# Gate and up products of the second token group in seven block products for eight

## The chip, the cores and the metric

One core of a Trainium2 chip runs the whole program in one launch. The metric is the device time of one launch in microseconds (us), lower is better. Each core has TensorE (PE, with its weight loads PEld), VectorE (DVE), ScalarE (ACT), GpSimd (POOL) and SyncE (SP), and 16 DMA engines that the queues of all of them feed. Every engine takes its instructions in order and waits on semaphores.

## What is computed

One layer of a streaming encoder on 1024 prompt tokens and 32 sample tokens (1056 columns of width D = 1024). Cut to what matters here:

```python
mix = concat([mlstm(h), fox_attention(h), gmlp(h)]) @ w_o
x = layer_norm(ALPHA * x + (1 + g1) * mix, ln1_g, ln1_b)
h = x * (1 + sc2) + sh2
y = (silu(h @ w_gate) * (h @ w_up)) @ w_down      # w_gate, w_up: 1024 x 2816; w_down: 2816 x 1024
x = layer_norm(ALPHA * x + (1 + g2) * y, ln2_g, ln2_b)
```

All of it is in 32-bit floats.

## The kernel before

Tokens lie on the free axis, features on the 128 partitions. The tokens form two groups, group 0 of 512 columns (two cuts of 256) and group 1 of 544 (two cuts of 272; its last 32 columns are the sample tokens): `GN`, `MM`, `LN`. A function's argument `c` is the group.

**Products.** Every matrix product is taken in three matmuls (`gemm`, L110 to L116): an operand is split into a rounded part `hi` and a rest `lo`, both of the type fp32r, and hi x hi, hi x lo and lo x hi are summed in PSUM. `weights()` (L91 to L106) loads 128 x 1024 floats into a `raw` buffer (3 of them, `RAW`), ACT casts it to `whi` (L102), DVE subtracts to `wlo` (L103; 3 buffers of each, `WB`). Activations are split likewise: `hh`/`hl` in the tiles `ah` and `al`, one pair for each cut, written by `ln1` (ACT L944, DVE L945).

**The FFN.** `w_gate` and `w_up` are cut into 22 tiles of 128 columns. `up(c, j)` computes tile j: for each cut a gate product into the PSUM pool `pg` (buffers `up_g`) and an up product into `pu` (`up_u`), 8 blocks of 128 rows x 3 matmuls each, so 4 x 24 = 96 matmuls of 272 columns a tile for group 1. Then ACT does Exp, Ln, Exp (silu's sigmoid) and DVE two multiplications (L990, L991), and `acth`/`actl` are split off (ACT L992, DVE L993). Tiles come in `GROUPS` of 3 or 4; after a group's tiles `down(c, g)` multiplies with its part of `w_down` and DVE adds each result to the residual `z` (L923). The first tile of the next group comes ahead of each down pass, to cover its start.

**Order in time** (`run`). Group 0's tiles and down passes are woven into the second half of the mixers (eight attention heads "fox", four "mlstm" heads; some 440 to 960 us of the span), since these leave PE free; POOL does the key sums `fm_qkr` (L365), the residual scaling of group 0's first LayerNorm (L954) and the mlstm heads' `mqb`, `mv`, `mo` there. SP issues all loads and stores in one queue (L85, L88). At some 905 us group 1's output projection and its `ln1` follow, from 1013 group 1's FFN pass: tiles 0 to 3, group 0's last LayerNorm (`ln2`, both cuts after tile 3), the down pass, and so on. The last group runs half by half: up products of cut 0, down of cut 0, `ln2` of cut 0, then the same for cut 1, with the gate and up weights loaded and split again. `last_weights` keeps the last part of `w_down` in the chip for both halves.

A scheduler turns the program's order into an order for each engine: a program text that is written in another order, or has more instructions, moves instructions on all of them. `issue_after` holds an instruction behind another one.

## Time and profile before

| what | value |
| --- | --- |
| runs | 1435.03, 1435.16, 1438.75 us (median 1435.16) |
| profiled execution | 1436.1 us, of it span 1434.3 us |
| mean granted PE clock | 0.986 |
| PE / DVE / ACT / POOL busy | 97% / 67% / 45% / 18% of the span |
| moved by DMA | 207.35 MB, mean 145 GB/s |

The profile's times count from the start of the span; a row names the line of the code, the engine, the operation, what it writes and reads, and how often, with its busy time and the mean of one in ns. PE's matmuls are pipelined: the mean of one overlaps with its neighbours, and the count in a stretch gives the pitch.

### The profile page before, as it was taken

The page shows a single profiled execution, that of the slowest core. Times are in us where ns is not written, and L with a number is a line of the kernel's source. Part 1 is how long each engine was busy: PE and PEld are TensorE (multiplying, and loading weights), DVE is VectorE, ACT ScalarE, POOL GpSimd, SP SyncE. Part 2 cuts the span into 40 slices and gives each one's busy share as a digit, 9 for nine tenths or more (in the row PEclk, how much of TensorE's full clock was granted, in tenths as well). Part 3 has the DMA queues.
Part 4 walks back from the last instruction along what each step waited for, and adds up shares of the span by engine and source line. Part 5 has one row for each costly group of instructions (what it writes and reads, how often), then busy time and mean ns, then how long its engine had stood idle before and what let it go on. Part 6 is the DMA issues. An engine that isn't in the chain of part 4 may idle for free.

```text
span 1434.3 us, 28877 instructions
## 1 busy us (share of the span) xinstructions
PE 1385.6 (97%) x11141; PEld 1336.3 (93%) x11141; DVE 960.7 (67%) x2220; ACT 641.3 (45%) x1405; POOL 254.3 (18%) x295
## 2 busy tenths in 40 slices
PE   7999999999999899999999999999999999999994
PEld 4899988989899889999999998999999999999994
DVE  5558655678688777687767765668857545454676
ACT  3323244434445564546555353436745342424353
POOL 0103100043157300000000002254500000000433
PEclk9999999999999999999999999999999999999997
DMA  9754678565654755443443533522224222222431
GB/s 359 253 210 128 200 206 259 160 197 168 224 176 151 215 161 178 115 145 120 126 139 104 101 104 67 196 89 74 100 73 153 89 89 89 89 89 89 133 104 63
DMA packets 120867, 207.35 MB, mean 145 GB/s; under 512 B 21380, under 2 KB 76300, under 8 KB 120728
## 3 DMA queue, kind: packets, MB, share of 16 engines
q1 hardware_dynamic: 120728, 205.49, 45.9%
q8 instruction: 88, 1.44, 0.4%
q14 instruction: 51, 0.42, 0.1%
HBM read 173.78 MB, written 31.66 MB: 143 GB/s over the span
## 4 chain that ended last, share of the span: by engine, by line
PE 82%; DMA 7%; DVE 6%; ACT 1%; issue 1%; SPq 1%; POOL 1%; DVEq 0%; ACTq 0%; POOLq 0%
PE up_g L115 8%; PE up_g L116 8%; PE up_g L114 8%; PE dn_g L114 4%; PE dn_g L115 4%; PE dn_g L116 4%; PE up_u L116 3%; PE up_u L115 3%; PE up_u L114 3%; PE tm_g L279 2%; PE tm_g L280 2%; PE tm_g L281 2%; PE fox_t L729 2%; PE wo_g L114 2%; PE wo_g L115 2%; PE wo_g L116 2%
## 5 line engine op out<-in xcount | busy, mean ns | idle before, releaser
L114 PE MATMUL up_g<-wo_ah,up_whi 128*128 128x256 f32 (+1 forms) x1008 | 288.8, 287 | 3.4 <-ACT lna_tmp L942 3.3
L115 PE MATMUL up_g<-wo_al,up_whi 128*128 128x256 f32 (+1 forms) x1008 | 290.4, 288 | 0.4 <-DVE wo_al L945 0.4
L116 PE MATMUL up_g<-wo_ah,up_wlo 128*128 128x256 f32 (+1 forms) x1008 | 289.4, 287 | 0.0
L114 PEld LDWEIGHTS up_g<-wo_ah,up_whi 128*128 128x128 f32 x1008 | 191.4, 190 | 4.9 <-ACT wo_ah L944 3.5
L115 PEld LDWEIGHTS up_g<-wo_al,up_whi 128*128 128x128 f32 x1008 | 191.6, 190 | 1.3 <-DVE wo_al L945 0.7
L116 PEld LDWEIGHTS up_g<-wo_ah,up_wlo 128*128 128x128 f32 x1008 | 191.3, 190 | 0.4 <-DVE up_wlo L103 0.2
L102 ACT CAST up_whi<-up_raw 128x1024 fp32r<-128x1024 f32 x94 | 98.5, 1047 | 143.1 <-PE dn_u L115 53.8
L103 DVE TENSOR_TENSOR up_wlo<-up_raw,up_whi 128x1024 fp32r<-128x1024 f32 x94 | 121.1, 1288 | 61.0 <-ACT up_whi L102 60.7
L114 PE MATMUL dn_g<-up_acth,dn_whi 128*128 128x256 f32 (+1 forms) x464 | 133.8, 289 | 2.4 <-DVE mlstm_z L923 2.4
L115 PE MATMUL dn_g<-up_actl,dn_whi 128*128 128x256 f32 (+1 forms) x464 | 132.3, 286 | 0.0
L116 PE MATMUL dn_g<-up_acth,dn_wlo 128*128 128x256 f32 (+1 forms) x464 | 132.1, 285 | 0.0
L116 PE MATMUL up_u<-wo_ah,up_wlo 128*128 128x272 f32 (+1 forms) x400 | 115.4, 289 | 0.0
L114 PE MATMUL up_u<-wo_ah,up_whi 128*128 128x272 f32 (+1 forms) x400 | 114.9, 287 | 0.0
L115 PE MATMUL up_u<-wo_al,up_whi 128*128 128x272 f32 (+1 forms) x400 | 114.5, 286 | 0.0
L280 PE MATMUL tm_g<-tm_wlo,start_h1h 128*128 128x256 f32 (+1 forms) x384 | 111.3, 291 | 0.0
L281 PE MATMUL tm_g<-tm_whi,start_h1l 128*128 128x256 f32 (+1 forms) x384 | 111.0, 290 | 0.0
L279 PE MATMUL tm_g<-tm_whi,start_h1h 128*128 128x256 f32 (+1 forms) x384 | 110.3, 289 | 0.2 <-ACT tm_mixs L630 0.2
L114 PE MATMUL fm_g<-start_h1h,fm_whi 128*128 128x256 f32 (+2 forms) x344 | 102.7, 304 | 5.5 <-ACT fm_whi L102 1.9
L115 PE MATMUL fm_g<-start_h1l,fm_whi 128*128 128x256 f32 (+2 forms) x344 | 102.5, 298 | 0.1
L116 PE MATMUL fm_g<-start_h1h,fm_wlo 128*128 128x256 f32 (+2 forms) x344 | 101.4, 296 | 0.0
L114 PEld LDWEIGHTS dn_g<-up_acth,dn_whi 128*128 128x128 f32 x464 | 87.7, 189 | 3.3 <-DVE mlstm_z L923 3.0
L115 PEld LDWEIGHTS dn_g<-up_actl,dn_whi 128*128 128x128 f32 x464 | 87.8, 189 | 0.4
(447 smaller groups left out, 3806.2 us busy)
## 6 DMA issues: line engine op xcount, KB each, us to landing
up_raw<-w_gu SPq DMA_DIRECT2D x94, 512.0 KB
dn_raw<-w_dn SPq DMA_DIRECT2D x30, 512.0 KB
ada_late<-w_ada SPq DMA_DIRECT2D x24, 512.0 KB
wo_raw<-w_o SPq DMA_DIRECT2D x24, 512.0 KB
ada_araw<-w_ada SPq DMA_DIRECT2D x16, 512.0 KB
fm_raw<-w_in_f SPq DMA_DIRECT2D x16, 512.0 KB
tm_raw<-w_in SPq DMA_DIRECT2D x12, 512.0 KB
dn_raw<-w_dn SPq DMA_DIRECT2D x16, 384.0 KB
```

The costliest lines, as they stand in the source:

```text
L102: nc.scalar.copy(hi[:, :w], raw[:, :w])
L103: (eng or nc.vector).tensor_tensor(lo[:, :w], raw[:, :w], f(hi[:, :w]), ALU.subtract)
L114: nc.tensor.matmul(ps, hi, xh(k), start=start and k == 0, stop=False)
L115: nc.tensor.matmul(ps, hi, xl(k), start=False, stop=False)
L116: nc.tensor.matmul(ps, lo, xh(k), start=False, stop=stop and k == n - 1)
L279: nc.tensor.matmul(ps[:, :ncol], xh, hi, start=k == 0, stop=False)
L280: nc.tensor.matmul(ps[:, :ncol], xh, lo, start=False, stop=False)
L281: nc.tensor.matmul(ps[:, :ncol], xl, hi, start=False, stop=k == 7)
L729: nc.tensor.transpose(ps[:, y * P:(y + 1) * P], probs[y][:, b * P:(b + 1) * P], self.ident)
```

## The change

Each gate and up pair of tile j is a product of a 2 x 2 block matrix of weights (rows 0 to 511 and 512 to 1023; gate columns and up columns) with a 2 x 2 block matrix of activations (the same rows; the two cuts). For group 1 and tiles 4 to 21 the change computes it by a scheme of seven block products (`sup`): 7 x 4 x 3 = 84 matmuls of 272 columns for 96. It needs three sums of weight blocks, and four combinations of the activations.

- The input `w_gu` holds for each tile the four blocks gate rows 0 to 511, gate rows 512 to 1023, up rows 0 to 511, up rows 512 to 1023, 512 columns each, side by side.
- `sums` makes the weight sums in DRAM, in `dp[j]` (128 x 4 x 512 for each tile): two copies from DRAM to DRAM of 512 KB, issued on SP (L92 of the changed code, the `store`), then three accumulating transfers in POOL's queue (L1017: 512, 256 and 256 KB), each of which waits for the one before. With `NS0 = 22` all of them are called in group 0's pass, one call after each tile of group 0, copies one step and additions up to three steps behind.
- `sup_operand` makes the four activation combinations: `ln1` of group 1 also stores its result in DRAM (`dh`, 16 stores on SP); after tile 3, 16 loads of 136 KB bring it back, with 32 DVE and 16 ACT operations; the combinations lie in the tiles `ah`/`al` that group 0 no longer needs.
- A new tile loads and splits 3.5 x 1024 columns of weights (two own blocks whole, one more own block, four blocks of sums) in place of 2 x 1024.
- Exp, Ln and Exp work on 544 columns; so does the tail of `sup` on DVE.
- Group 0's `ln2` cuts come after tiles 1 and 2. In the last group the new tiles 19 to 21 are done whole, then the two halves' down passes and LayerNorms; the weights of all four units of that down pass are loaded ahead of both.

```diff
+FF = 22
+SJ = 4
+NS0 = 22
...
+            if c:
+                self.store(self.dh[:, k, sl], h)
...
+    def sums(self):
+        nc = self.nc
+        i = self.nsum
+        self.nsum += 1
+        add = lambda out, x: nc.gpsimd.dma_start(out, x, accum_op=ALU.add)
+        blocks = lambda j: self.d["w_gu"][j].rearrange("p (b n) -> p b n", b=4)
+        if i < FF:
+            b = blocks(i)
+            with self.tc.issue_after(self.lastload.ins):
+                self.store(self.dp[i][:, 0:2], b[:, 2:3].to_broadcast([P, 2, 512]))
+                self.store(self.dp[i][:, 2:4], b[:, 0:2])
+        j = i - 1
+        if SJ <= j < FF:
+            add(self.dp[j][:, 0:2], blocks(j)[:, 0:4:3])
+        j = i - 2
+        if SJ <= j < FF:
+            add(self.dp[j][:, 2], self.dp[j][:, 1])
+        j = i - 3
+        if SJ <= j < FF:
+            add(self.dp[j][:, 3], self.dp[j][:, 2])
...
+    def sup_operand(self, ks):
...
+        for k in ks:
+            for r in (k, k + 4):
+                for t in (0, 272):
+                    x = self.t(self.p2, [P, 272], F32, "tmp", 4)
+                    self.load(x, self.dh[:, r, t:t + 272])
...
+            nc.vector.tensor_tensor(b22, b22, b12, ALU.subtract)
+            nc.vector.tensor_tensor(b12, b11, b12, ALU.subtract)
+            nc.vector.tensor_tensor(b11, b22, b11, ALU.add)
+            nc.vector.tensor_tensor(b21, b11, b21, ALU.subtract)
+            for i, x in ((1, b11), (0, b12), (2, b22), (3, b21)):
+                nc.scalar.copy(self.T[i][0][:, k], x)
+                nc.vector.tensor_tensor(self.T[i][1][:, k], x, f(self.T[i][0][:, k]), ALU.subtract)
...
+    def sup(self, j, act, pool):
...
+        w1 = self.weights(self.d["w_gu"][j][:, :1024], KT, P)
+        w2 = [self.t(self.px, [P, 512], F32R, x, 1) for x in ("w2h", "w2l")]
...
+        w3, w4 = (self.weights(self.dp[j][:, i:i + 2].rearrange("p b n -> p (b n)"), KT, P) for i in (2, 0))
...
+        nc.scalar.copy(u1, prod(w1[:4], own(0, 0)))
+        tt(x[:, a], prod(w1[4:], own(0, 4)), u1, ALU.add)
+        tt(uv[:, a], u1, prod(w3[:4], com(1)), ALU.subtract)
+        tt(uv[:, b], prod(w4[4:], com(0)), uv[:, a], ALU.add)
+        tt(x[:, b], prod(w3[4:], own(272, 4)), uv[:, b], ALU.add)
+        s = self.t(self.p2, [P, 544], F32, "sil", 2)
+        nc.scalar.activation(s, x, AF.Exp, scale=-1.0)
+        nc.scalar.activation(s, s, AF.Ln, bias=self.one)
+        nc.scalar.activation(s, s, AF.Exp, scale=-1.0)
+        tt(s, x, s, ALU.mult)
+        tt(two(c), prod(w4[:4], com(2)).unsqueeze(1).to_broadcast([P, 2, 272]), two(uv), ALU.add)
+        tt(c[:, a], prod(blocks(w2, 0), com(3)), c[:, a], ALU.add)
+        nc.vector.scalar_tensor_tensor(c, c, -1.0, s, ALU.mult, ALU.mult)
+        nc.scalar.copy(ah, c)
+        tt(al, c, f(ah), ALU.subtract)
...
+                if j >= SJ:
+                    self.sup(j, act, pa)
+                    continue
                 weave(self.up(1, j, act, pa, MM[1]))
+                if 0 < j < 3:
+                    self.ln2(0, self.st0, *LN[0][j - 1], "vpvvpvvp", "aaaaaaaa")
+                if j == 3:
+                    weave(self.sup_operand(range(4)))
...
         for half, (a, b) in enumerate(LN[1]):
-            for j in range(j0 + 1 + (half and UPF), j0 + nj):
-                weave(self.up(1, j, (act, act2)[half], pa, ((a, b),)))
...
+            self.down(1, last, act, ((a, b),), st, w)
             self.ln2(1, st, a, b, TADD[half], TAFF[half])
```

What this does to the engines' orders, at three places. POOL, in the start of the mixers' second half (the residual scaling of group 0's LayerNorm, L954, in the changed code L962, and the key sums, L365, now L371), before:

```order
114 L954 TENSOR_SCALAR mlstm_z_837_4328<-mlstm_z_837_4328,start_colp_88 128x256 [waits Activation_49] x4
115 L365 TENSOR_TENSOR fm_qkr_6143<-fm_qkh_6141,fm_qkl_6142 128x272 [waits DMAHW2_49,DVE_49]
116 L370 COPY start_qks_137<-fm_qkr_6143 128x32 [waits Pool_49]
117 L365 TENSOR_TENSOR fm_qkr_6184<-fm_qkh_6182,fm_qkl_6183 128x272 [waits DMAHW2_49,DVE_49]
118 L954 TENSOR_SCALAR mlstm_z_837_4328<-mlstm_z_837_4328,start_colp_88 128x256 [waits Activation_49] x2
```

The same place after (`start_dp_13` is `dp[4]`, the sums of the first new tile; DMASW is the semaphore of a transfer in POOL's queue, DMAHW of one of SP's):

```order
112 L371 TENSOR_TENSOR fm_qkr_6128<-fm_qkh_6126,fm_qkl_6127 128x272 [waits DMAHW7_49,DVE_49]
113 L1017 DMA start_dp_13_69<-w_gu 128x2x512 [waits DMAHW3_49]
114 L945 TENSOR_TENSOR mlstm_z_856_4347<-mlstm_z_856_4347,wo_qs_5375 128x256 [waits DVE_49] x2
115 L962 TENSOR_SCALAR mlstm_z_856_4347<-mlstm_z_856_4347,start_colp_107 128x256 [waits Activation_49]
116 L1017 DMA start_dp_13_69<-start_dp_13_69 128x512 [waits DMAHW4_49,DMASW0_49]
117 L962 TENSOR_SCALAR mlstm_z_856_4347<-mlstm_z_856_4347,start_colp_107 128x256 [waits Activation_49] x3
118 L371 TENSOR_TENSOR fm_qkr_6162<-fm_qkh_6160,fm_qkl_6161 128x272 [waits DMAHW2_49,DVE_49]
119 L371 TENSOR_TENSOR fm_qkr_6203<-fm_qkh_6201,fm_qkl_6202 128x272 [waits DMAHW2_49,DVE_49]
120 L376 COPY start_qks_156<-fm_qkr_6162 128x32 [waits Pool_49]
121 L962 TENSOR_SCALAR mlstm_z_856_4347<-mlstm_z_856_4347,start_colp_107 128x256 [waits Activation_49]
122 L1017 DMA start_dp_13_69<-start_dp_13_69 128x512 [waits DMASW1_49]
```

Three additions with waits of their own stand between instructions that followed each other directly.

SP, the loads around group 1's first down pass and the tiles after it, before:

```order
700 L85 DMA dn_raw_14516<-w_dn 128x768 [waits DMAHW0_49,DVE_49]
701 L85 DMA dn_raw_14568<-w_dn 128x768 [waits DMAHW1_49,DVE_49]
702 L85 DMA dn_raw_14620<-w_dn 128x768 [waits DMAHW2_49,DVE_49]
703 L85 DMA dn_raw_14672<-w_dn 128x768 [waits DMAHW3_49,DVE_49]
704 L85 DMA up_raw_14726<-w_gu 128x1024 [waits DMAHW4_49,DVE_49]
705 L85 DMA up_raw_14732<-w_gu 128x1024 [waits DMAHW5_49,DVE_49]
```

After (`sup_tmp` are the loads for the combinations; `sup_raw` of numbers 15048 to 15066 are the weights of tile 5, the second new one):

```order
777 L88 DMA sup_tmp_14662<-start_dh_68 128x272 [waits DMAHW1_49,DVE_49,Activation_49]
778 L88 DMA sup_raw_15060<-start_dp_14_70 128x1024 [waits DMAHW2_49,DMASW5_49,DMAHW5_49,DMASW4_49,DVE_49]
779 L88 DMA sup_tmp_14664<-start_dh_68 128x272 [waits DVE_49]
780 L88 DMA sup_tmp_14666<-start_dh_68 128x272 [waits DMAHW4_49,DVE_49]
781 L88 DMA sup_raw_15066<-start_dp_14_70 128x1024 [waits DMAHW7_49,DMASW3_49,DVE_49]
782 L88 DMA sup_tmp_14668<-start_dh_68 128x272 [waits DMAHW6_49,DVE_49]
783 L88 DMA sup_tmp_14682<-start_dh_68 128x272 [waits DVE_49,Activation_49]
784 L88 DMA sup_tmp_14684<-start_dh_68 128x272 [waits DMAHW0_49,DVE_49]
785 L88 DMA sup_tmp_14686<-start_dh_68 128x272 [waits DMAHW1_49,DVE_49]
786 L88 DMA sup_tmp_14688<-start_dh_68 128x272 [waits DMAHW2_49,DVE_49]
```

The loads of the last combinations stand behind weight loads of a later tile, in a queue that held weights alone.

DVE, one tile in the middle of group 1's pass, before:

```order
1773 L990 TENSOR_TENSOR up_sil_15516<-up_g_15466,up_sil_15516 128x272
1774 L991 TENSOR_TENSOR up_sil_15516<-up_u_15491,up_sil_15516 128x272
1775 L993 TENSOR_TENSOR up_actl_15453<-up_sil_15516,up_acth_15452 128x272
1776 L103 TENSOR_TENSOR up_wlo_15593<-up_raw_15590,up_whi_15592 128x1024
1777 L990 TENSOR_TENSOR up_sil_15574<-up_g_15524,up_sil_15574 128x272
1778 L991 TENSOR_TENSOR up_sil_15574<-up_u_15549,up_sil_15574 128x272
1779 L103 TENSOR_TENSOR up_wlo_15717<-up_raw_15714,up_whi_15716 128x1024
1780 L993 TENSOR_TENSOR up_actl_15453<-up_sil_15574,up_acth_15452 128x272
```

After, one new tile (its last operation, on 544 columns, comes behind the next tile's first ones, as row 1826 does here):

```order
1824 L107 TENSOR_TENSOR sup_wlo_15803<-sup_raw_15800,sup_whi_15802 128x1024
1825 L1094 TENSOR_TENSOR sup_uv_15690<-sup_tmp_15688,sup_u_15720 128x272
1826 L1107 TENSOR_TENSOR sup_actl_15527<-sup_c_15555,sup_acth_15526 128x544
1827 L1095 TENSOR_TENSOR sup_uv_15690<-sup_g_15734,sup_uv_15690 128x272
1828 L1096 TENSOR_TENSOR sup_sil_15689<-sup_u_15748,sup_uv_15690 128x272
1829 L107 TENSOR_TENSOR sup_wlo_15815<-sup_raw_15812,sup_whi_15814 128x1024
1830 L1103 TENSOR_TENSOR sup_c_15691<-sup_g_15767,sup_uv_15690 128x544
1831 L107 TENSOR_TENSOR sup_wlo_15821<-sup_raw_15818,sup_whi_15820 128x1024
1832 L1104 TENSOR_TENSOR sup_c_15691<-sup_u_15781,sup_c_15691 128x272
1833 L1074 TENSOR_TENSOR sup_w2l_15807<-sup_raw_15808,sup_w2h_15806 128x512
1834 L1101 TENSOR_TENSOR sup_sil_15762<-sup_sil_15689,sup_sil_15762 128x544
1835 L1105 SCALAR_TENSOR_TENSOR sup_c_15691<-sup_c_15691,sup_sil_15762 128x544
```

Eight operations become thirteen, with three and a half weight splits among them in place of two.

More of the change, by code (lines that the diff above doesn't have):

```diff
@@ L84, in load, with weights @@
     def load(self, out, in_):
-        return self.nc.sync.dma_start(out, in_)
+        self.lastload = self.nc.sync.dma_start(out, in_)
+        return self.lastload
     def store(self, out, in_):
         self.nc.sync.dma_start(out, in_)
-    def weights(self, src, nk, ncol, eng=None):
+    def weights(self, src, nk, ncol, eng=None, keep=None):
         nc = self.nc
@@ L975, in up @@
         ah, al = act[j] = [self.t(pool, [P, GN[c]], F32R, x, 5) for x in ("acth", "actl")]
-        w = [self.weights(self.d["w_gu"][2 * j + i], KT, P) for i in range(2)]
+        w = [self.weights(self.d["w_gu"][j][:, i * 1024:(i + 1) * 1024], KT, P) for i in range(2)]
         for a, b in cuts:
@@ L1067, in run @@
         self.dd0 = t([4, 9], "dd0")
+        self.dh = t([P, KT, GN[1]], "dh")
+        self.dp = {j: t([P, 4, 512], f"dp{j}") for j in range(SJ, FF)}
+        self.T = []
+        self.nsum = SJ
         self.dmix = [t([P, KT, GN[c]], f"dmix{c}") for c in range(2)]
@@ L1233, in run @@
         act = {}
-        for g, (j0, nj) in enumerate(GROUPS[:-1]):
-            for j in range(j0 + (g > 0), j0 + nj + 1):
-                weave(self.up(1, j, act, pa, MM[1]))
-            if g == 0:
-                for a, b in LN[0]:
-                    self.ln2(0, st, a, b, "vpvvpvvp", "aaaaaaaa")
-            st = self.ln_begin(nc.gpsimd, sum=False) if g == last - 1 else None
-            self.down(1, g, act, MM[1], st)
+        self.px = self.pool("px")
+        for g, (j0, nj) in enumerate(GROUPS):
+            for j in range(j0 + (g > 0), j0 + nj + (g < last)):
+                if self.nsum < FF + 3:
+                    self.sums()
+                if j >= SJ:
+                    self.sup(j, act, pa)
+                    continue
+                weave(self.up(1, j, act, pa, MM[1]))
+                if 0 < j < 3:
+                    self.ln2(0, self.st0, *LN[0][j - 1], "vpvvpvvp", "aaaaaaaa")
+                if j == 3:
+                    weave(self.sup_operand(range(4)))
+            if g < last:
+                st = self.ln_begin(nc.gpsimd, sum=False) if g == last - 1 else None
+                self.down(1, g, act, MM[1], st)
         st.update(pivot=False, sum=True, order=(4, 5, 6, 7, 0, 1, 2, 3))
-        j0, nj = GROUPS[-1]
         n = nj * 256
```

63 lines of the change are left out of this document (51 added, 12 removed).

## Prediction

> **What bounds the kernel now.** First the head of the page: the busy shares, the slices and the DMA kinds.
>
> ```profile
> PE 1385.6 (97%) x11141; PEld 1336.3 (93%) x11141; DVE 960.7 (67%) x2220; ACT 641.3 (45%) x1405; POOL 254.3 (18%) x295
> DVE  5558655678688777687767765668857545454676
> POOL 0103100043157300000000002254500000000433
> PEclk9999999999999999999999999999999999999997
> DMA  9754678565654755443443533522224222222431
> q1 hardware_dynamic: 120728, 205.49, 45.9%
> PE 82%; DMA 7%; DVE 6%; ACT 1%; issue 1%; SPq 1%; POOL 1%; DVEq 0%; ACTq 0%; POOLq 0%
> ```
>
> TensorE is busy for 97% of the span and carries 82% of the chain that ended last, at full clock. So matmuls taken out are worth their time, if nothing else then ends last. From slice 28 on (group 1's FFN pass) DVE stands at 4 to 5 tenths and the DMA engines at 2: room for the added work, on average. All data moves through one kind of queue, which the hardware issues; there is no row for a DMA from POOL's queue, for one from DRAM to DRAM, or for one that accumulates.
>
> Second the stretches of the span (us, busy and count of PE, PE's loads, DVE, ACT, POOL; clock, DMA share, GB/s): six of group 1's FFN pass, then the stages from which POOL and SP get new work, then the end.
>
> ```profile
> 1013.00:1062.00 49.00, 49.00 (x393) 48.95 (x392) 30.08 (x53) 28.67 (x62) 11.54 (x11) 1.00 0.25 80
> 1062.00:1080.00 18.00, 18.00 (x141) 17.84 (x140) 17.31 (x42) 10.18 (x19) 2.44 (x3) 1.00 0.45 144
> 1080.00:1092.00 12.00, 12.00 (x98) 12.00 (x98) 11.97 (x28) 5.20 (x10) 2.44 (x3) 1.00 0.35 124
> 1150.00:1175.00 25.00, 25.00 (x202) 25.00 (x201) 10.32 (x17) 11.10 (x21) 0.00 (x0) 1.00 0.28 86
> 1200.00:1225.00 25.00, 25.00 (x202) 25.00 (x201) 11.19 (x20) 8.89 (x15) 0.00 (x0) 1.00 0.28 96
> 1300.00:1325.00 25.00, 25.00 (x202) 25.00 (x202) 10.03 (x16) 10.88 (x20) 0.00 (x0) 1.00 0.28 85
> 440.00:465.00 25.00, 24.96 (x193) 24.42 (x192) 20.43 (x40) 15.01 (x32) 17.29 (x18) 1.00 0.43 140
> 465.00:480.00 15.00, 11.25 (x81) 10.56 (x80) 14.79 (x30) 7.95 (x19) 9.12 (x11) 0.89 0.61 190
> 480.00:500.00 20.00, 20.00 (x158) 19.05 (x158) 10.91 (x31) 10.80 (x27) 5.24 (x10) 0.91 0.92 246
> 520.00:860.00 340.00, 339.52 (x2800) 334.60 (x2793) 255.40 (x646) 179.26 (x438) 5.71 (x13) 1.00 0.44 127
> 1392.00:1415.00 23.00, 22.64 (x181) 22.42 (x180) 18.17 (x43) 11.45 (x24) 8.34 (x9) 1.00 0.15 50
> 1415.00:1434.00 19.00, 1.19 (x4) 0.68 (x4) 11.06 (x24) 5.25 (x10) 4.58 (x6) 0.60 0.17 60
> ```
>
> In group 1's pass PE never stops and does 202 matmuls of 272 columns in 25 us: 123.8 ns each. (A group's mean of 288 ns overlaps its neighbours; the pitch is the price.) In 465 to 480 PE stands still for a quarter of the time and in 480 to 500 the DMA engines are at 0.92: that is where new transfers have no room.
>
> **The saving.** Each of the 18 tiles does 84 matmuls for 96: 216 x 0.1238 = 26.7 us less PE time. A tile takes 84 x 0.1238 = 10.40 us in place of 11.88.
>
> **DVE inside a new tile.** Durations from group 1's stretch, 960 to 1434:
>
> ```profile
> L103 DVE TENSOR_TENSOR up_wlo<-up_raw,up_whi 128x1024 fp32r<-128x1024 f32 x53 | 69.8, 1316 | 46.6 <-ACT up_whi L102 46.6
> L102 ACT CAST up_whi<-up_raw 128x1024 fp32r<-128x1024 f32 x53 | 55.5, 1046 | 99.6 <-PE dn_u L115 53.8 <-PE up_g L115 30.8 <-PE up_u L115 5.1
> L990 DVE TENSOR_TENSOR up_sil<-up_g,up_sil 128x272 f32<-128x272 f32 (+1 forms) x48 | 21.0, 438 | 35.3 <-ACT up_sil L989 33.6
> L993 DVE TENSOR_TENSOR up_actl<-up_sil,up_acth 128x272 fp32r<-128x272 f32 (+1 forms) x48 | 22.2, 462 | 11.6 <-ACT up_acth L992 11.5
> L988 ACT ACTIVATE up_sil<-up_sil,start_ones 128x272 f32<-128x272 f32 (+1 forms) x48 | 25.1, 522 | 1.4
> L923 DVE SCALAR_TENSOR_TENSOR wo_z<-dn_u,start_mod,wo_z 128x240 f32<-128x240 f32 (+2 forms) x72 | 26.6, 399 | 21.8 <-PE dn_u L116 20.3 <-POOL wo_z L920 1.3
> L938 DVE TENSOR_TENSOR wo_z<-wo_z,wo_pv 128x272 f32<-128x272 f32 x16 | 8.2, 574 | 0.0
> L945 DVE TENSOR_TENSOR wo_al<-lna_tmp,wo_ah 128x272 fp32r<-128x272 f32 x16 | 7.6, 500 | 0.2 <-ACT wo_ah L944 0.2
> ```
>
> Between 272 columns (438 ns) and 1024 (1316 ns) lies 1.17 ns a column, so 544 columns come to about 755 ns and 512 to 718: estimates from these two rows. Before, a tile has 2 splits of 1316 and 6 operations of about 450 ns: 5.3 us. After, 3 splits of 1024 (3.95), one of 512 (0.72), five operations of 272 (2.2) and four of 544 (3.0) make 9.9 us, 95% of PE's 10.40. ACT has 3 x 1046, 0.6, 0.4 for the copy of the first product, three passes and a cast of 544 (2.5 to 3): under 7 us, hidden. The loads grow from 1 MB to 1.75 MB a tile; 86 GB/s went with a share of 0.28, so 1.75 MiB (1.83 MB) in 10.4 us, 176 GB/s, is a share near 0.57: hidden.
> With DVE at 95% PE waits only where order and buffers let it; three raw and three split buffers and three or more PSUM tiles a pool give DVE a few microseconds of lag. I take 0.2 us a tile, 4 us in all; from 0 to 14 (0.8 us a tile, if the added SBUF-to-SBUF operations cost what L938's 574 ns costs against 438, and each end of a tile is waited for).
>
> **The combinations of the activations.** Sixteen loads, 32 DVE operations (16 as L938 and 16 as L945: 9.2 + 8.0 = 17.2 us) and 16 ACT casts lie between tile 3 and the first new tile, with the down pass of units 0 to 2. From the first tile to the end of that down pass (1013 to 1080) DVE is busy for 30.08 + 17.31 = 47.4 of 67 us. Group 0's second LayerNorm, which ran on past 1080 (11.97 of 12 us busy to 1092), now starts a tile or two earlier, so that some 9 us of it come into that stretch; with the 17.2 and the first new tile's larger splits (4.7 us for 2.6) DVE has 76 us to do in 67: about 9 us late. By the instruction orders, the loads of the last two combination steps are moreover queued on SP behind the fourth weight block of tile 5, whose buffer frees only after the first products of tile 4; PE then has two products that need no combination (3 us) and waits for a split (2 x 1.2), a load and eight DVE operations of some 0.5 us for each of two steps. Counted so, the stall is again about 9 us: 3 + 2.4 + 2 x 4 + 1.5 less what PE still has, some 6. One delay, two counts: 9 us, from 2 (DVE catches up while PE does the eight products without new operands) to 14. Behind the waiting SP loads stand tile 5's and 6's weights, which then are late by the same time, not by more. The 16 stores of the new operand in ln1 (each 136 KB, in a stretch of DMA share 0.27) keep a buffer of four until they land; L938 and POOL's L954 there give 0 to 2 us, taken 1.
>
> **The weight sums.** 36 SP copies and 54 POOL additions are queued between 440 and 960. Bytes first: 1 MB of copies and 1 MB of additions for each of 18 tiles, 36 MB in 400 us is 94 GB/s beside 127 at a share of 0.44, so a share of 0.8 if they cost as loads do; PE's stretch 520 to 860 has DMA room. Where not:
>
> ```profile
> POOL mlstm_mqb L522 <- PE mlstm_s L549: 204.4, 4, 62.0
> 453.62 5.92 POOL mlstm_z L954 x4
> 475.41 0.94 POOL mlstm_z L954
> 477.15 2.56 POOL mlstm_z L954 x2
> 479.70 0.74 POOL fm_qkr L365
> 486.35 5.29 DMA fox_v<-start_dv
> 491.66 5.08 DMA mlstm_mb<-start_dM
> ```
>
> The first row is POOL's waiting from 540 on: 204 us in four waits, so an addition that holds POOL there holds nobody. The chain of waits at 453 to 497 is the opposite: L954 and L365 on POOL end it, then loads in full DMA engines. The additions of the first new tile stand between exactly these POOL instructions, each waiting for the one before, and the next copies ahead of the loads of the attention head. The nearest row for a 512 KB transfer is fox_v's 5.29 us under load; at the 246 GB/s of 480 to 500 it is 2.1 us. Two waits of POOL at 2 to 5 us less the POOL slack, and 1 MB of copies ahead of the head's loads at 2 to 5 us: I take 5 us. Later heads start on loads that SP issues just before use; there I take 1. Ends for both: 0, and 25, if every addition takes the 7.4 us (400 / 54) at which POOL has no slack left and its waits go through to the heads. A gain is excluded: nothing is removed there.
>
> The Trainium skill, "DMA: Bandwidth & Descriptors", on the anatomy of one DMA, gives a software-queued transfer about 2 us fixed and then bytes over 436 GB/s: an estimate of 3.2 us for 512 KB. By it the sum would stay as it is; no row here shows such a queue. The same page says that queues of different engines share the same 16 DMA engines, and the row 480 to 500 with 0.92 is what speaks against putting more there.
>
> **The end.** Before, the last group runs half by half, so the first half's LayerNorm (pieces of 8 x L938's kind) lies under the second half's gate and up products. After, the products of tiles 19 to 21 come first and only the second half's down pass (96 matmuls and a few, 12 to 13 us) covers it. DVE's work there: the second half's 8 residual additions in two pieces (some 0.53 a pair, L923's kind), 8 sums of squares (0.5) and 16 operations of the first half's normalisation (0.54, between L945 and L938): 4.2 + 4.0 + 8.6 = 16.8 us over PE's 11.9 to 13. So the end comes some 3.6 us later; 0 (POOL takes a share) to 7. That the second half's gate and up weights are no longer loaded and split again gains nothing: PE is at 22.64 of 23 us there before.
>
> **Sum.** -26.7 + 4 (new tiles) + 9 (combinations) + 1 (stores) + 5 + 1 (sums) + 3.6 (end) = -3.1 us. Against the profiled execution's 1436.1 (span 1434.3 and 1.8 around it) that is 1433.0; the median of the runs is 0.9 lower, so 1432.1. About 4.3 us (0.3%) is what a measurement of this kernel can tell from no change, and this sum lies inside it, as the middle of a forecast that leans to faster: four of the six costs are late starts, which PE partly makes up when its buffers run full again. I put 1431.
>
> **The rivals.**
> A, nearly all arrives. The four POOL waits of 204 us and DVE's mean of 45% in group 1 hide the new work, and only the end, half of the combinations and 2 us of all else remain: -26.7 + 4.5 + 3.6 + 2 = -16.6, 1418.6. Against it: DVE's 17.31 of 18 us just where the combinations go.
> B, slower: the additions take longer than 7.4 us each. POOL's in-order queue then falls behind its mixers' work and SP's copies wait ahead of the heads' loads; at 8.4 us it is 54 us of POOL time, of which the heads' starts (8) would pass perhaps 3 us each, 24 us, on top of the sum's other -9: 1450. It decides from about 8 us an addition; fox_v's 5.29 us for 512 KB, plus an addition's second read, comes near it.
> C, DVE sets the new tile. If its operations sum to 11.1 us, not 9.9 (L103's three stay, the ten others at 5.95 us are 20% dearer; L938 is 31% dearer than L990), a tile takes 11.1 and the saving shrinks to 18 x 0.78 = 14 us; with the other costs (19.6) that is +5.6, 1441. For it: the 95% above; against it: the wider operations pay their start once.
> The Trainium skill, "SBUF — State Buffer", in its trap on DVE blocking DMA, says that software-queued descriptors can starve while DVE holds the shared port. As a mechanism here: DVE is busy for 255 of 340 us in 520 to 860, so an addition that gets only the free quarter takes four times its 2 us, 8 us, which is B's threshold. It is part of B's chance.
>
> **Chances.** Forecast (1424 to 1438) 0.47; A 0.20; B 0.20; C 0.13. The range reaches from A to B's near edge, 1414 to 1449. Faster by over 4.3 us: all of A and half of the forecast less a little, 0.43; within: 0.27; slower: B, most of C, 0.30.
>
> **What would show it.** In the changed kernel: 84 matmuls and 10.4 to 10.7 us a new tile with PE near 100% (if 11 or more and DVE full: C); one PE gap of about 9 us before the third product of tile 4, with the chain through SP, a load of the combination and DVE; PE gaps near 453 to 500 that grew by about 5 us, behind POOL's additions; mixers otherwise as before (PE gaps at each head: B); the last matmul to the end 3 to 4 us longer. The forecast fails if a DRAM-to-DRAM addition costs more than the loads' rows allow, or if the combinations are hidden.

## The result: 39 us slower

The changed kernel takes 1475.23 us (median of 4 runs, 1471.53 to 1478.12) against 1435.84 for the kernel before, measured with it: 1.0269 times, 95% interval 1.0236 to 1.0303. The forecast was 1431, with 1414 to 1449 around it. The profiled execution is the slowest of its four, 1478.12 us with a span of 1476.3, so 42.0 us of span are to be found.

The page of the changed kernel, in the rows that answer to those shown of before:

```profile
PE 1378.6 (93%) x10925; PEld 1324.6 (90%) x10925; DVE 1028.7 (70%) x2336; ACT 659.5 (45%) x1397; POOL 301.3 (20%) x349
PEclk9999999999999899999999989899999899999996
DMA  9754768664756988879789773442435444335331
q1 hardware_dynamic: 137144, 239.84, 50.8%
q0 software_dynamic: 10080, 18.88, 9.2%
PE 73%; DMA 14%; DVE 7%; ACT 2%; issue 2%; SPq 1%; POOL 1%; DVEq 0%; ACTq 0%; POOLq 0%
start_dp<-w_gu POOLq DMA_DIRECT2D x18, 512.0 KB, 9.3
start_dp<-start_dp POOLq DMA_DIRECT2D x36, 256.0 KB, 6.3
```

PE does 216 matmuls less and yet is busy for a smaller share; DMA's part of the chain doubles from 7% to 14%. The DMA slices 15 to 24, some 510 to 870 us, go from 3 to 5 tenths to 7 to 9. The new queue moved 18.88 MB, the additions, and its packets took 9.2% of the span of 16 engines: 136 us, 7.2 us a MB. The other queue's 239.84 MB took 750 us, 3.1 us a MB. An addition of 512 KB lands after 9.3 us, one of 256 KB after 6.3.

Where group 1's FFN pass begins, and how its stages go on, stands in the timeline of PE (start, duration, operation; after an idle time its length and releaser; rows picked out). Before, the first gate product of tile 0:

```profile
1013.46 0.29 PE L114 MATMUL up_g<-wo_ah,up_whi 128*128 128x272 f32 x1
```

After, the same product, the start of new tiles 4 to 6 and of the down pass behind them, then of tiles 7 to 10 and the down pass behind those; and the wait at the end:

```profile
1063.90 0.29 PE L120 MATMUL up_g<-wo_ah,up_whi 128*128 128x272 f32 x1
1131.75 0.29 PE L120 MATMUL sup_g<-wo_ah,sup_whi 128*128 128x272 f32 x1
1176.83 0.29 PE L120 MATMUL dn_g<-up_acth,dn_whi 128*128 128x272 f32 x1
1194.99 0.29 PE L120 MATMUL sup_u<-wo_ah,sup_whi 128*128 128x272 f32 x1
1237.04 0.29 PE L120 MATMUL dn_g<-sup_acth,dn_whi 128*128 128x272 f32 x1
1458.12 1.28 PE L860 MATMUL lnb_t<-sup_zs,start_onesm 128*128 128x272 f32 x2 [6.97 <-POOL sup_zs L851]
```

So the pass starts 50.4 us late, and this delay builds up in the stages in which the sums are made. The same products of the heads, before and after:

| first product of PE in | before | after | late by |
| --- | --- | --- | --- |
| the first attention head of the mixers' second half | 487.78 | 495.17 | 7.4 |
| the fifth of its heads | 660.75 | 693.69 | 32.9 |
| the last | 800.98 | 836.78 | 35.8 |
| the attention of the sample tokens | 861.64 | 909.10 | 47.5 |
| group 1's FFN pass | 1013.46 | 1063.90 | 50.4 |

Tiles 7 to 10 take 42.05 us in place of the 48.1 of four tiles at the old pace, close to the 41.6 forecast. Tiles 4 to 6 take 45.1 where 31.5 would be three times that pace: 13.5 us are lost there. From the end of the last down pass to the end of the span it takes 25.2 us in place of 19.7, 5.5 us longer. With the 27.2 us that 18 shorter tiles save, 50.4 + 13.5 + 5.5 - 27.2 gives 42.2, the 42.0 to be found.

The stretches of the changed kernel (columns as above: us, PE, PE's loads, DVE, ACT, POOL, clock, DMA share, GB/s):

```profile
440.00:860.00 420.00, 388.76 (x3050) 376.48 (x3049) 289.72 (x730) 204.36 (x499) 79.74 (x97) 0.95 0.85 211
1113.00:1177.00 64.00, 55.34 (x405) 54.42 (x405) 51.48 (x106) 32.18 (x56) 0.86 (x1) 0.89 0.49 155
1195.00:1237.00 42.00, 42.00 (x338) 42.00 (x337) 32.63 (x50) 24.20 (x34) 0.00 (x0) 1.00 0.48 164
```

Before, 440 to 860 reads:

```profile
440.00:860.00 420.00, 415.46 (x3380) 405.94 (x3379) 316.29 (x783) 225.47 (x547) 37.37 (x50) 0.99 0.47 137
```

PE does 3050 matmuls there in place of 3380, at a DMA share of 0.85 for 0.47, and the clock falls with the gaps. In 1195 to 1237 PE is full, and DVE is busy for 32.63 of 42 us, 78% and not 95%.

What crowded DMA engines do to PE is seen in the chain of waits of the changed kernel, 589 to 607 (start, us, what; pieces picked out):

```profile
589.32 0.89 SPq L92
590.30 12.55 DMA mlstm_mo<-start_dmo
602.93 0.42 ACT mlstm_mo L541
603.38 0.52 ACT mlstm_mo L542
604.24 1.04 ACT up_whi L106
606.74 0.33 DVE up_sil L1000
```

SP issues copies for the sums (L92), then a small load of 128 x 256 for an mlstm head, and this takes 12.55 us; ACT, in order, holds the cast of FFN weights behind it, and PE stands still for 4.0 us.

A second way leads through POOL. The chain at 846 to 877, the matmul that ends it in PE's timeline, and DVE's wait there:

```profile
846.02 8.41 DMA start_dp<-w_gu
854.71 12.22 DMA start_dp<-w_gu
867.21 4.70 DMA start_dp<-start_dp
872.20 0.47 POOL start_dp L1017
873.44 1.05 POOL foxs_q L767
876.46 0.34 DVE fox_ptl L739
876.84 0.48 PE L740 MATMUL fox_o<-fox_ptl,fox_v 128*64 128x256 f32 x1 [9.76 <-DVE fox_ptl L739]
DVE foxs_q L768 <- POOL foxs_q L767: 12.3, 1, 12.3
```

POOL waits for a copy, issues an addition of 512 KB, waits until it has landed, and so on to the next; the clearing of `foxs_q` (L767) for the sample tokens' attention stands behind these in its order. DVE waits 12.3 us for it, with the work of the attention heads behind, and PE stands still for 9.8 us. This is the longest of PE's waits from 440 to 1000, which sum to 43.5 us, against 6.9 before.

### The profile page after: what moved, and what is told of

It reads as the page before. It is cut to its first block, busy times and chain, and to the rows that moved or that the text cites. A ratio compares the mean times of both kernels' runs of the same rounds, so it can differ in the third digit from the quotient of the medians.

```text
span 1476.3 us, 28949 instructions
## 1 busy us (share of the span) xinstructions
PE 1378.6 (93%) x10925; PEld 1324.6 (90%) x10925; DVE 1028.7 (70%) x2336; ACT 659.5 (45%) x1397; POOL 301.3 (20%) x349
## 3 DMA queue, kind: packets, MB, share of 16 engines
q1 hardware_dynamic: 137144, 239.84, 50.8%
q0 software_dynamic: 10080, 18.88, 9.2%
## 4 chain that ended last, share of the span: by engine, by line
PE 73%; DMA 14%; DVE 7%; ACT 2%; issue 2%; SPq 1%; POOL 1%; DVEq 0%; ACTq 0%; POOLq 0%
PE up_g L120 4%; PE up_g L121 4%; PE up_g L122 4%; PE dn_g L120 3%; PE dn_g L121 3%; PE dn_g L122 3%; DMA start_dp<-w_gu 3%; PE tm_g L285 3%; PE tm_g L286 3%; PE tm_g L287 3%; PE sup_u L122 2%; PE sup_u L121 2%; PE sup_u L120 2%; PE fm_g L120 2%; PE fm_g L121 2%; PE fm_g L122 2%
## 5 line engine op out<-in xcount | busy, mean ns | idle before, releaser
L120 PE MATMUL up_g<-wo_ah,up_whi 128*128 128x256 f32 (+1 forms) x720 | 209.4, 292 | 11.6 <-DVE up_sil L1000 4.0
L121 PE MATMUL up_g<-wo_al,up_whi 128*128 128x256 f32 (+1 forms) x720 | 209.8, 292 | 0.5 <-DVE wo_al L953 0.5
L122 PE MATMUL up_g<-wo_ah,up_wlo 128*128 128x256 f32 (+1 forms) x720 | 208.2, 290 | 0.0
L120 PEld LDWEIGHTS up_g<-wo_ah,up_whi 128*128 128x128 f32 x720 | 139.7, 194 | 14.4 <-DVE up_sil L1000 4.2
L121 PEld LDWEIGHTS up_g<-wo_al,up_whi 128*128 128x128 f32 x720 | 140.2, 195 | 1.3 <-DVE wo_al L953 0.8
L122 PEld LDWEIGHTS up_g<-wo_ah,up_wlo 128*128 128x128 f32 x720 | 140.0, 195 | 0.3
L106 ACT CAST sup_whi<-sup_raw 128x1024 fp32r<-128x1024 f32 x54 | 56.7, 1050 | 110.9 <-PE dn_u L121 59.8
L107 DVE TENSOR_TENSOR up_wlo<-up_raw,up_whi 128x1024 fp32r<-128x1024 f32 x52 | 66.4, 1277 | 34.6 <-ACT up_whi L106 34.3
L120 PEld LDWEIGHTS fm_g<-start_h1h,fm_whi 128*128 128x128 f32 x344 | 66.6, 195 | 15.7 <-DVE fm_qkl L370 6.2
L1017 POOL DMA_DIRECT2D start_dp<-start_dp x36 | 30.4, 844 | 234.1 <-DMA start_dp<-w_gu 119.4
L107 DVE TENSOR_TENSOR sup_wlo<-sup_raw,sup_whi 128x1024 fp32r<-128x1024 f32 x54 | 66.0, 1223 | 14.7 <-ACT sup_whi L106 14.7
```

Of the source, the lines that this page charges most:

```text
L106: nc.scalar.copy(hi[:, :w], raw[:, :w])
L107: (eng or nc.vector).tensor_tensor(lo[:, :w], raw[:, :w], f(hi[:, :w]), ALU.subtract)
L120: nc.tensor.matmul(ps, hi, xh(k), start=start and k == 0, stop=False)
L121: nc.tensor.matmul(ps, hi, xl(k), start=False, stop=False)
L122: nc.tensor.matmul(ps, lo, xh(k), start=False, stop=stop and k == n - 1)
L1017: add = lambda out, x: nc.gpsimd.dma_start(out, x, accum_op=ALU.add)
```

## The experiments

All were timed in three rounds against the kernel before on the same chip; the table has medians and the ratio to before with its 95% interval. The medians of the kernel before were 1435.8 to 1438.9 us in these measurements, so a few us between rows are better read from the ratios. "Start" is the first product of group 1's FFN pass, in the profiled execution.

| run | us | ratio | start |
| --- | --- | --- | --- |
| changed kernel | 1475.2 | 1.0269 (1.0236 to 1.0303) | 1063.9 |
| no_sums | 1423.7 | 0.9909 (0.9874 to 0.9945) | 1011.3 |
| no_adds | 1431.5 | 0.9953 (0.9934 to 0.9972) | 1021.8 |
| plain_copies | 1446.4 | 1.0066 (1.0039 to 1.0092) | 1032.4 |
| late_adds | 1481.5 | 1.0302 (1.0262 to 1.0341) | 1065.3 |
| sp_copies | 1454.2 | 1.0116 (1.0099 to 1.0132) | 1042.5 |
| sp_copies2 | 1490.1 | 1.0349 (1.0317 to 1.0381) | 1081.1 |
| no_sums_early | 1422.7 | 0.9901 (0.9883 to 0.9919) | 1014.6 |
| pool_sums3_early | 1496.8 | 1.0415 (1.0393 to 1.0438) | 1013.7 |
| ns0_11 | 1471.6 | 1.0245 (1.0222 to 1.0269) | 1037.3 |
| ns0_0 | 1487.9 | 1.0354 (1.0306 to 1.0403) | 1018.9 |
| pool_z | 1433.0 | 0.9976 (0.9960 to 0.9992) | 1016.7 |
| pool_z_mid | 1420.2 | 0.9882 (0.9854 to 0.9911) | 1017.2 |

The theory: the sums' transfers fill the DMA engines in 440 to 960, and every load there is late. The rival: POOL is held by the waits of its additions, and what stands behind them is late. The trace spoke for both: POOL waited 219 us for the copies and 75 for earlier additions.

### No sums at all

```diff
+        return
...
-        w3, w4 = (self.weights(self.dp[j][:, i:i + 2].rearrange("p b n -> p (b n)"), KT, P) for i in (2, 0))
+        w3, w4 = (self.weights(self.d["w_gu"][j][:, i * 512:i * 512 + 1024], KT, P) for i in (2, 0))
```

The `return` stands at the head of `sums`: no copy and no addition.

> Leaves out the weight sums: no copy and no addition in DRAM; the new tiles load blocks of w_gu of the same size in their place (so its output is not the layer's). The trace of the changed kernel has group 1's FFN pass begin 50 us later than before (1063.9 against 1013.5). Both theories, that the DMA engines are full in 440 to 960 and that POOL is held by the waits of the additions, expect that start back at 1013 to 1018. Left are the 26.7 us of matmuls saved, the stall at the combinations (13.5 us) and the longer end (5 us): 1435.8 - 26.7 + 13.5 + 5 + 2 = 1429, from 1424 to 1434. A third theory, that the layout of the weights or the stores of the operand slow the mixers, expects 1450 or more.

1423.7 us, and the start is back at 1011.3, 52.6 us earlier: weights' layout and the operand's 16 stores cost nothing that can be seen. The sums cost 51 us. What is left is 0.991 of before, some 13 us better, where the matmuls alone give 27.

### Copies without additions

```diff
-        add = lambda out, x: nc.gpsimd.dma_start(out, x, accum_op=ALU.add)
+        add = lambda out, x: None
```

> Leaves out the 54 additions and keeps the 36 copies from DRAM to DRAM (its output is not the layer's). If the additions are most of it, by their engine time (the software queue took 9.2% of 16 engines' span, 136 us, for 18.9 MB) or by holding POOL: within 10 us of the kernel without sums, near 1435. If bytes alone count, copies and additions alike: half way, 1450 to 1455.

1431.5: the additions are 44 of the 51 us, the copies 8, for the same bytes written.

### The same transfers as plain copies

```diff
-        add = lambda out, x: nc.gpsimd.dma_start(out, x, accum_op=ALU.add)
+        add = lambda out, x: nc.gpsimd.dma_start(out, x)
```

> The 54 transfers in POOL's queue copy and do not accumulate (its output is not the layer's); bytes written, waits and queue are the same, the second read is gone. If accumulation is what makes them slow (139 GB/s over the time of their packets, against 312 GB/s for the other queue): a time nearer to the kernel without additions, 1440 to 1455, and a software queue well below 9.2%. If the queue or the copies from DRAM to DRAM are: 1468 to 1480.

1446.4. Same queue, bytes and order of waits, without the accumulation: 29 us of the 44 go. The software queue and the landing times of the page of this run:

```profile
q0 software_dynamic: 5472, 18.88, 4.7%
start_dp<-w_gu POOLq DMA_DIRECT2D x18, 512.0 KB, 6.6
start_dp<-start_dp POOLq DMA_DIRECT2D x36, 256.0 KB, 4.6
```

4.7% of 1444.2 is 68 us, against 136: adding costs the engines twice what copying does (and 10080 packets for 5472). PE's wait behind POOL at `foxs_q` is 4.0 us here, in place of 9.8.

### Additions issued later

```diff
-        j = i - 1
+        j = i - 2
...
-        j = i - 2
+        j = i - 4
...
-        j = i - 3
+        j = i - 6
...
-                if self.nsum < FF + 3:
+                if self.nsum < FF + 6:
```

> The same transfers, but an addition is issued 2, 4 and 6 tiles after the copies in place of 1, 2 and 3, so that POOL finds what it waits for long landed. If POOL's waits (219 and 75 us in the trace) are the cause: within 10 us of the kernel without additions, some 1440. If the full DMA engines are: no better than the changed kernel, 1468 to 1480.

1481.5, like the changed kernel. But this does not decide between the theories. The scheduler placed the additions so that POOL waits as before, in this run's waits from 440 to 1000:

```profile
POOL start_dp L1017 <- DMA start_dp<-w_gu: 206.2, 26, 25.9
POOL start_dp L1017 <- DMA start_dp<-start_dp: 97.6, 17, 11.1
```

The edit changed the program's order and not the wait, so the next two kernels take POOL out of it. PE's wait behind POOL at `foxs_q` grew to 14.3 us.

### Traffic without POOL

```diff
-        add = lambda out, x: nc.gpsimd.dma_start(out, x, accum_op=ALU.add)
+        def add(out, x, j, s, n):
+            with self.tc.issue_after(self.lastload.ins):
+                for dq in self.dq[j]:
+                    self.store(dq[:, s:s + n], x)
...
```

with one scratch `dq[j]` for each tile, or two; these copies read blocks of `w_gu`.

> In place of the 54 additions, 54 copies of the same size from w_gu to a scratch that nothing reads, issued on SP and waiting for nothing: traffic without POOL (its output is not the layer's). The kernel with later additions did not settle whether POOL's waits matter, since they stayed (206 and 98 us). If the full DMA engines are the cause: as the copies in POOL's queue, 1443 to 1450. If POOL's being held is: as the kernel without additions, 1428 to 1435.

> The same with every one of these copies made twice, to two scratches. Packet time of 54 plain copies was 4.7% of 1444 us (68 us), of 54 additions 9.2% of 1476 (136 us), so 108 copies hold the DMA engines as long as the additions do, with POOL free. Full DMA engines as the cause: 1462 to 1482, like the changed kernel. POOL's waits as the cause: below 1445.

1454.2 and 1490.1: 23 and 59 us over the kernel without additions, with nothing on POOL, and both above the range given for full engines. So a loss as large as the whole one needs no wait of POOL. But one copy of each cost 8 us more than the same bytes in POOL's queue (1446.4): SP's queue, in which they stand ahead of the heads' loads, has a part in these two, and they don't show that the engines' share alone does it. Nor do they clear POOL in the changed kernel: no PE wait behind `foxs_q` is in their traces, and there it is 9.8 us. How much of the 44 us comes through POOL's order, and how much through late loads, no run separates.

The time follows what the transfers hold of the engines. The shares of the hardware and software queues, times the span, are 709 us without sums, 775 with the copies alone, 838 with plain copies, 850 with SP's copies, 886 in the changed kernel and 922 with SP's copies twice; the medians stand in the same order. The stretch 440 to 860 in the kernels without additions, with plain copies, with SP's copies once and twice, each a run of its own:

```profile
440.00:860.00 420.00, 410.22 (x3322) 401.01 (x3320) 311.32 (x772) 222.18 (x540) 38.56 (x51) 0.99 0.62 180
```

```profile
440.00:860.00 420.00, 401.43 (x3196) 389.75 (x3195) 301.69 (x756) 215.74 (x525) 65.51 (x103) 0.97 0.75 220
```

```profile
440.00:860.00 420.00, 392.69 (x3135) 382.89 (x3134) 299.79 (x750) 210.39 (x516) 36.33 (x50) 0.98 0.77 213
```

```profile
440.00:860.00 420.00, 381.89 (x2972) 367.87 (x2972) 283.15 (x700) 198.49 (x480) 36.90 (x48) 0.96 0.85 238
```

With the share at 0.47, 0.62, 0.75, 0.77, 0.85, 0.85, PE's matmuls there fall from 3380 over 3322, 3196, 3135 and 3050 (the changed kernel) to 2972. There is no threshold at 1: in this kernel the loss starts well below a full share, as a mean over the stretch, and grows with it. At 0.85 the two counts differ by 78, so the share is not all.

### The sums in the other pass

```diff
-NS0 = 22
+NS0 = 11
```

and `NS0 = 0`.

> The whole layer; half of the calls that make the weight sums come in group 0's pass, half in group 1's (NS0 = 11). If the cost comes from full DMA engines in 440 to 960 and grows with their share (0.59 there cost 8 us, 0.74 some 21, 0.85 some 48): the share there falls to about 0.65, some 12 us, and group 1's goes from about 0.45 to 0.75: with a few us lost there 1438 to 1450, a clear gain over 1475. If the cost were fixed for each addition: no change, 1470.

> All sums in group 1's pass (NS0 = 0): group 1's FFN begins at 1010 to 1018 as in the kernel without sums. There the additions' 136 us and the copies' 60 or so come on top of a share of about 0.45 over 350 us: 1.0. If full engines are the limit wherever they stand: a loss of 15 to 60 us in group 1's pass, 1440 to 1480, with gaps before the splits. If group 1's regular loads, ahead by three buffers, can wait: 1424 to 1432.

1471.6 and 1487.9. My estimate of 1438 to 1450 for the half was a miss. Three stretches of that run, from the last down pass of group 0 to tile 6:

```profile
1007.00:1037.00 30.00, 24.83 (x193) 23.98 (x192) 22.41 (x48) 13.58 (x29) 6.98 (x8) 0.95 0.83 189
1037.00:1120.00 83.00, 69.87 (x530) 68.93 (x529) 64.05 (x118) 44.58 (x95) 28.22 (x37) 0.92 0.82 205
1120.00:1170.00 50.00, 37.42 (x260) 36.20 (x259) 33.80 (x67) 20.36 (x35) 5.69 (x6) 0.83 0.83 214
```

The sums of the second half are not spread over group 1's pass; they are made as a lump in 1007 to 1170, share 0.82, where LayerNorms and combinations need their loads too. So the loss moved with them. With all of them there the time is above the 1440 to 1480 that I gave for this case, the share in 1150 to 1350 is 0.92, and PE also waits for the splits of the new tiles:

```profile
1150.00:1350.00 200.00, 186.23 (x1399) 181.66 (x1397) 125.31 (x215) 75.44 (x102) 29.79 (x31) 0.97 0.92 232
```

Neither half nor all of them in the other pass is hidden at 7.2 us a MB.

### The late combinations

```diff
-                if 0 < j < 3:
-                    self.ln2(0, self.st0, *LN[0][j - 1], "vpvvpvvp", "aaaaaaaa")
-                if j == 3:
-                    weave(self.sup_operand(range(4)))
+                if j < 2:
+                    weave(self.sup_operand(range(2 * j, 2 * j + 2)))
+                else:
+                    self.ln2(0, self.st0, *LN[0][j - 2], "vpvvpvvp", "aaaaaaaa")
```

on the kernel without sums.

> The kernel without sums (other weights in their place, its output is not the layer's), with the activation combinations made after tiles 0 and 1 and group 0's last LayerNorm after tiles 2 and 3. Its trace had gaps of 5.0 and 2.9 us and a low clock in the first new tiles, 12.2 us over the later pace of three tiles. If the late combinations are that stall: 1423.7 - 11 = 1413, from 1410 to 1416, and no gap over 1 us from 1000 to 1380. If DVE's work just moves the stall: 1419 to 1425.

1422.7, no measurable gain. The one PE gap over 1 us left in these tiles is of 1.2. From the start of tile 0 to the down pass behind tile 6 it takes 106.4 us (1014.6 to 1121.1) against 111.2 (1011.3 to 1122.5) with the late combinations: 4.8 of the 11.9 us lost there are gone, the rest went into many short waits, most of them for DVE, busy for 104.5 of the 120 us from 1000 on. This execution also started that pass 3.4 us later, for which the traces show no cause.

### The sums on the chip

POOL makes the sums from blocks that lie in SBUF, so each new tile loads 1 MB. In place first, in the raw buffers `r1` and `r2`, once the blocks have been split (the combinations stay early, as in the kernel above):

```diff
...
+        w1 = split(r1)
+        w2 = split(r2[:, 512:], True)
+        sa = (nc.gpsimd, nc.gpsimd, nc.gpsimd, nc.gpsimd)
+        sa[0].tensor_tensor(r2[:, 512:], r2[:, :512], r2[:, 512:], ALU.add)
+        sa[1].tensor_tensor(r2[:, :512], r1[:, :512], r2[:, :512], ALU.add)
+        sa[2].tensor_tensor(r1[:, :512], r1[:, :512], r2[:, 512:], ALU.add)
+        sa[3].tensor_tensor(r1[:, 512:], r1[:, 512:], r1[:, :512], ALU.add)
+        w3 = split(r1)
+        w4 = split(r2)
```

> The whole layer, with the weight sums made on the chip: each new tile loads its four blocks once (1 MB in place of 1.75), and POOL makes the four sums in place, 128 x 512 each, once the blocks have been split; combinations early as in the kernel beside it. POOL's rows of 256 columns take 0.85 us, so four of 512 some 6.8 us of a tile's 10.4. If that and the three raw buffers are hidden: 1410 to 1418. If the chain load, split, sum, split through three buffers is longer than a tile, or POOL and DVE slow each other: 1.5 us a tile or more, 1438 to 1460.

1496.8, above even the range given for a chain that is too long: the start is in time, but four tiles take 57 to 59 us. The groups from 1150 to 1300 say why:

```profile
L1084 POOL TENSOR_TENSOR sup_raw<-sup_raw 128x512 f32<-128x512 f32 x8 | 11.9, 1488 | 108.4 <-DVE sup_w2l L1078 108.4
```

POOL's first sum waits 108.4 us, 13.6 a tile, for a split whose only buffer frees with the tile's last product. The next kernel keeps the four blocks of two tiles in group 0's residual tile and writes the sums elsewhere:

```diff
+        if j == SJ:
+            self.zr = self.t(self.pz, [P, 2, 2048], F32, "z0", 1)
+        r = self.zr[:, j % 2]
...
+        s4, s3 = (self.t(self.wp, [P, 1056], F32, "raw", RAW)[:, :1024] for _ in range(2))
+        add = lambda e, *x: e.tensor_tensor(*x, ALU.add)
+        add(nc.gpsimd, s4[:, 512:], r[:, 1024:1536], r[:, 1536:])
+        add(nc.gpsimd, s3[:, :512], r[:, :512], s4[:, 512:])
+        add(nc.gpsimd, s3[:, 512:], r[:, 512:1024], s3[:, :512])
+        add(nc.gpsimd, s4[:, :512], r[:, :512], r[:, 1024:1536])
```

> The whole layer, sums on the chip by POOL, but not in place: group 0's residual tile, free after its last LayerNorm, holds the four blocks of two tiles, and the sums go to two of the three raw buffers. In the kernel with sums in place POOL waited 108 us for the split of the last block (8 tiles), which waits for TensorE's last product; that wait is gone. POOL's four sums were 1.33 to 1.49 us each there, 5.6 us of a tile's 10.4. If that chain was the cause: within 6 us of the kernel without sums, 1424 to 1430, faster than both. If POOL and DVE slow each other (DVE's 544-column operations took 958 ns beside POOL): 1440 or more.

1433.0, a little above the 1424 to 1430 given for it: that chain was most of the loss, and this is the whole layer at about the time of before. The combinations come late again here. The last kernel moves group 0's LayerNorm to tiles 0 and 1 and the combinations to tiles 1 and 2:

```diff
-                if 0 < j < 3:
-                    self.ln2(0, self.st0, *LN[0][j - 1], "vpvvpvvp", "aaaaaaaa")
-                if j == 3:
-                    weave(self.sup_operand(range(4)))
+                if j < 2:
+                    self.ln2(0, self.st0, *LN[0][j], "vpvvpvvp", "aaaaaaaa")
+                if 0 < j < 3:
+                    weave(self.sup_operand(range(2 * j - 2, 2 * j)))
```

> The same, with group 0's last LayerNorm after tiles 0 and 1 and the combinations after tiles 1 and 2: a step earlier than in the changed kernel. If DVE's total work up to the first new tile sets the stall: no more than 5 us better than the kernel beside it. If the order on SP and DVE does: 8 to 12 us better.

1420.2, 0.988 of before (0.985 to 0.991): 1.2% shorter, with the whole layer computed. From the start of tile 0 to the down pass behind tile 6 it takes 107.1 us against 117.0, so 10 of the 12.8 us are the stall at the combinations, and in this kernel their order was its cause more than DVE's total. In the kernel without sums, with another order, moving them gained nothing. Two stretches of this run:

```profile
1150.00:1350.00 200.00, 200.00 (x1594) 199.84 (x1593) 167.75 (x243) 89.55 (x123) 87.82 (x62) 1.00 0.30 95
440.00:860.00 420.00, 414.84 (x3370) 404.57 (x3369) 313.92 (x781) 224.18 (x547) 35.67 (x49) 0.99 0.47 135
```

PE is full in the new tiles, the DMA share is back at 0.30, and the mixers' 3370 matmuls are close to the 3380 of before. DVE is the busiest after PE, 84% there.

## Why the prediction was wrong

**The saving** was right: 84 matmuls a tile and 10.51 us a tile measured (42.05 / 4) for 10.40 forecast and 12.02 (48.1 / 4) before; 27 us in 18 tiles.

**The weight sums** are the step that failed: "36 MB in 400 us ... a share of 0.8 if they cost as loads do; PE's stretch 520 to 860 has DMA room", 5 us for the first head and 1 us for the later ones, at most 25. Measured: 51 us. The first head came 7.4 us late, so that term was near; what was mis-sized is the 1 us for all that follows, where the start of group 1's pass came another 43 us late. Three things in it were wrong. The additions do not cost as loads do: 136 us of the engines for 18.9 MB, where the plain copies of the same bytes took 68; the prediction named this among the signs that it fails. A mean share of 0.8 (0.77 by the prediction's own figures, 0.85 measured) is not room: at 0.62 the stage already lost 58 matmuls of 3380, and in the changed kernel, at 0.85, a load of an mlstm head, issued just before its use, took 12.55 us, and ACT, in order, held FFN work behind it. And "an addition that holds POOL there holds nobody" did not hold: at 846 to 874 POOL's wait for its additions held DVE for 12.3 us and PE for 9.8. The row that should have said so was among those quoted: the chain at 453 to 497 ended in loads at a share of 0.92. I took it as one place, and loads of the heads were late at several more once the share rose.

**Rival B** had the sign, with a chance of 0.20, and a size of 24 us for the heads; additions landed after 9.3 and 6.3 us, near its 8. Both halves of its mechanism are in the trace: POOL behind its work at `foxs_q`, and SP's copies ahead of an mlstm head's load. What it lacked is the size, and that POOL is not needed for it: copies on SP with POOL free lost as much. The rule quoted from the Trainium skill, "DMA: Bandwidth & Descriptors", on the anatomy of one DMA, gave an estimate of 3.2 us for 512 KB in the software queue; the trace has 9.3 in a crowded stage, so the measurement decides against that estimate there. The other sentence quoted from this page of the Trainium skill, that the queues of different engines share the same 16 engines (section "Issuing engines are not separate DMA queues"), is what the runs agree with: copies in either queue lengthened the kernel (1446.4 us in POOL's, 1454.2 in SP's, 1431.5 without them). The rule of the Trainium skill, "SBUF — State Buffer", in its trap on DVE blocking DMA, is stated there for DVE operations in a two-port mode, and the prediction took it for all of DVE's busy time. No run here isolates it; what the runs show is that the engine time doubled with the accumulation in the same queue.

**The combinations**: forecast 9 us (2 to 14), measured 13.5 in the changed kernel and 11.9 in the one without sums. PE's two gaps stood before the matmuls of the third and of the fourth combination step, those whose loads are queued behind weights on SP, as told:

```profile
1144.34 0.59 PE L120 MATMUL sup_g<-up_al,sup_whi 128*128 128x272 f32 x1 [5.66 <-ACT up_al L1059]
1150.05 0.59 PE L120 MATMUL sup_g<-up_al,sup_whi 128*128 128x272 f32 x1 [3.00 <-ACT up_al L1059]
```

The low clock about them (0.89 in 1113 to 1177) was missing from the sum.

**DVE in a new tile**: forecast 95% and 4 us, measured 78% and none. The mean of 1316 ns for a split, from a stretch in which POOL works too, was 1224 in the new tiles; operations on 544 columns took 718, not 755.

**The end**: forecast 3.6, measured 5.5. The prediction's own terms, 16.8 us of DVE over 11.9 to 13 of PE, give 3.8 to 4.9. PE waits 6.97 us for POOL's part of the last sums.

## What to carry to other kernels

A share of the DMA engines is not a budget to be filled: where loads are issued just before use, price added traffic by what a late load stops; here losses were seen from a mean share of 0.62 on. Ask also what stands behind a transfer in the order of the engine that issues it and waits for it. Ask what a transfer does, not only how many bytes it moves: here an accumulating one held the engines twice as long as a copy. If an engine idles beside the data, as POOL did in group 1's pass, a sum on the chip can be cheaper than a sum in memory, provided that nothing it reads is tied to a buffer that frees at the tile's end.

## What was not expected of the hardware

DVE's splits of 128 x 1024 took 1224 ns in the changed kernel's new tiles and 1590 ns where POOL added at the same time, in the last kernel's groups from 1160 to 1360, POOL's sums themselves 1.54 to 1.61 us beside it and 1.33 to 1.49 in the kernel in which POOL mostly waited:

```profile
L1084 POOL TENSOR_TENSOR sup_raw<-sup_z,sup_raw 128x512 f32<-128x512 f32 x24 | 38.7, 1610 | 33.7 <-DVE sup_wlo L1080 32.8
L1080 DVE TENSOR_TENSOR sup_wlo<-sup_raw,sup_whi 128x1024 fp32r<-128x1024 f32 x24 | 38.2, 1590 | 4.4 <-ACT sup_whi L1079 4.4
```

The mean hides two sizes. In the timeline of this stretch the splits of POOL's sums took 1.22 us where POOL was idle throughout (13 of 24) and 1.96 where it was busy throughout (8 of 24). DVE's operations that read a PSUM tile were not longer beside POOL: the product's addition (L1121, 272 columns) took 0.43 us in both cases, while one that reads two SBUF tiles (L1118, 544 columns) took 0.71 and 1.40. So operations with both inputs in SBUF were the slower ones here, and the change still paid as a whole.
